# Turning one token tile of the attention weights by VectorE block transposes and small SBUF copies, for seven of eight head pairs

## The chip, the core and the metric

The kernel runs on one core of a Trainium2 chip. The metric is the device time of one execution in microseconds (us). TensorE multiplies, VectorE, ScalarE and GpSimdE work on rows of 128 partitions, SyncE (SP) issues the transfers. On a profile page they are PE (with PEld for its weight loads), DVE, ACT, POOL and SP; L1251 is line 1251 of the kernel.

## The reference

The model has two layers, a pooling mixer and an attention layer, each followed by a squared-ReLU MLP, for 512 tokens of 1024 features. The change is in the attention layer, which has 16 heads of 64:

```
for i in range(S // Q_BLOCK):                 # four blocks of 128 queries
    z = q_blk @ k_blk.T / sqrt(64)            # keys 0 .. 128*(i+1)
    log1m = where(s < t, -softplus(z), 0)
    excl = cumsum_from_the_right(log1m) - log1m
    a = where(s < t, exp(log_sigmoid(z) + excl), 0)
    out_i = a @ v_blk
m = concat(out_i over heads) @ w_o
```

The attention is causal, so the block of queries i meets i+1 blocks of 128 keys: 1 + 2 + 3 + 4 = 10 blocks of 128x128 weights a for each head.

## The kernel before

The 512 tokens are four tiles of 128 (T = 4), the heads eight pairs. For each head the weights of all ten blocks stand side by side in one row of 1280 columns, tokens on the partitions; `SEG` says where a token tile starts: tile 3 (the last one) has columns 0 to 511, tile 2 512 to 895, tile 1 896 to 1151, tile 0 1152 to 1279.

One pair p goes through these steps, named by letters in the list `ATT_ORDER`, which is the order written out by hand for all five engines:

- `S`: 24 score products into six PSUM banks (PE, L1202), three for each head.
- `G`: sigmoids of both heads (ACT, L1216 and L1220).
- `X`, `M` for each head: a scan over the 1280 columns (DVE, L1225), and a multiplication that gives the weights w (DVE, L1316).
- `T` for each head: `transposed` turns the ten blocks w by PE against an identity (L1241), so that keys stand on the partitions, in three PSUM banks, and ACT copies the banks to tiles `at` (L1243).
- `A`: `mix_pair` multiplies v by the turned weights (PE, L1251), both heads side by side in the array, four block rows s of 512, 384, 256 and 128 columns. `a` takes the result out (ACT a cast, then DVE a subtraction, L414 and L415).
- Between them stand `J` and `Q`, the projections of the pair after (24 products each, L842 to L844), `j` and `q`, which split their results in a high part (ACT) and a low part (DVE L415), and work on weights that are loaded late: `L` loads (SP, L223), `g` scales by a gain (DVE, L230), `W` takes the high part (ACT, L249), `w` the low part (DVE, L258). An `L` waits until the `w` that last read its buffer is done, and what stands behind it on SP waits too.

On PE, pair p runs as S(p), J(p+1), Q(p+1), A(p-1), T(p), and then S(p+1). Pair 0 has other work in these places: S0, J1, V4, T0, Q1, V6, where V4 and V6 are products for v (L1126). V6 goes on in the banks of V4, which DVE has to read first (`v4`, L1142). Of DVE's work, `F4` (L1096, L1097 and a split) makes an operand for V6. After pair 6 come S7 and at once A6.

Of the kernel before, what the change touches and what calls it, by code (L numbers as in the profile page):

```python
# [10 lines left out]
F32 = mybir.dt.float32  # L11
# [4 lines left out]
P = 128  # L16
D = 1024
S = 512
T = S // P
KC = D // P  # L20
# [8 lines left out]
PAIRS = HEADS // 2  # L29
WINDOWS = (2, 4, 8, 16)  # L30
EPS = 1e-6
TS = [slice(t * P, (t + 1) * P) for t in range(T)]
NS = [slice(0, 512), slice(512, 1024)]
# [21 lines left out]
ATT_ORDER = [  # L55
    (w[0], int(w[1:2] or 0), int(w[2:] or 0))
    for w in """V5 N2 v5 V0 N3 V3 F3 v0 J0 v3 F2 j0 Q0 L L q0 V1 v1 F1 L L V2 v2
    S0 G0 X00 M00 J1 W X01 w V4 M01 j1 T00 T01 W F4 v4 w Q1 q1 V6 v6
    S1 G1 g g X10 M10 X11 J2 L L M11 W j2 w Q2 q2 A0 a0 T10 T11 W
    S2 G2 g g w X20 M20 X21 J3 M21 W j3 w L L Q3 q3 A1 a1 T20 T21 W  # L60
    S3 G3 g g w X30 M30 X31 J4 M31 W j4 w L L Q4 q4 A2 a2 T30 T31 W
    S4 G4 g g w X40 M40 X41 J5 M41 W j5 w L Q5 q5 A3 a3 T40 T41 W
    S5 G5 w L L X50 M50 X51 J6 M51 W j6 w L Q6 q6 A4 a4 T50 T51 W
    S6 G6 w X60 M60 X61 J7 M61 W j7 w L L L Q7 q7 A5 a5 T60 T61 W
    S7 A6 G7 w L X70 Z002 M70 W X71 w Z102 M71 W T70 w R a6 W w L W Z034 Z134 w T71 L W w L Z055 Z155
    W w L A7 W w Z066 Z166 z206 a7 W w s""".split()
]
# [23 lines left out]
def trunk(ctx, tc, x, consts, gcol, grow, pw, wup, wdn, wq, wk, wv, wo, out):  # L91
    nc = tc.nc
# [9 lines left out]
    def name(s):  # L102
        uid[0] += 1
        return f"{s}{uid[0]}"

    def ps():
        return psum.tile([P, 512], F32, tag="ps", name=name("ps"))
# [13 lines left out]
    turn = [0]  # L121
# [15 lines left out]
    behind, latest = {}, {}  # L137
# [19 lines left out]
    def gains(lo, n):  # L157


        def scaled(raw):  # L160
            for k in range(n):
                c = raw[:, k * D // n : (k + 1) * D // n]
                nc.scalar.mul(c, c, gc[:, lo + k : lo + k + 1])

        return scaled
# [44 lines left out]
    def late_next(what, fits=lambda x: True):  # L210
        while not fits(late[upto[what]]):
            upto[what] += 1
        upto[what] += 1
        return late[upto[what] - 1]
# [8 lines left out]
        nc.sync.dma_start(raw, x["src"])  # L223
        x["raw"] = raw

    def late_scale():
        x = late_next("g", lambda x: x["wide"] is not None)
        c = x["raw"].rearrange("p (k c) -> p k c", k=KC)
        g = gc[:, x["wide"] : x["wide"] + KC].unsqueeze(2).broadcast_to((P, KC, D // KC))
        nc.vector.tensor_tensor(out=c, in0=c, in1=g, op=ALU.mult)  # L230
# [134 lines left out]
    def fill(n=1):  # L365
        if gate[0]:
            behind.update(latest)
        for _ in range(n):
            if queue and sum(map(in_ring, made)) < ahead and (queue[0][0][0] != "dn" or dn_pool[0]):
                if not any(x["key"] == queue[0][0] for x in late) or queue[0][0] in kept:  # L370
                    make()
# [6 lines left out]
    for l in range(2):  # L378
        if l == 1:
            n = len(queue)  # L380
            for what, i, part in ATT_ORDER:
                if what == "V":
                    for h in range(2):
                        at = VALUES[i][2]
# [82 lines left out]
    class Update:  # L467
# [33 lines left out]
        def product(self, n):  # L501
            return self.beside if n and self.cuts is not NS else self.scaled
# [344 lines left out]
    with tc.tile_pool(name="mix0", bufs=1, reuse_waits="tile") as mp:  # L847
# [163 lines left out]
        def transposed(t, h):  # L1011
            pt = pts[t, h] = ps()
            for c in range(4):
                k = 4 * h + c
                nc.tensor.transpose(pt[:, TS[c]], xns[t][:, k * P : (k + 1) * P], ident)
# [47 lines left out]
    with tc.tile_pool(name="att", bufs=1, reuse_waits="tile") as ap:  # L1063
# [164 lines left out]
            )  # L1228
            return e

        def transposed(w):
            parts = {}
            for tiles in ((0,), (1, 3), (2,)):
                pt = ps()
                c = 0
                turned = ap.tile([P, S], F32, tag="at", bufs=6, name=name("at"))
                for s in tiles:
                    parts[s] = turned, c
                    for i in range(s, T):
                        at = SEG[i][0] + s * P  # L1240
                        nc.tensor.transpose(pt[:, c : c + P], w[:, at : at + P], ident)  # L1241
                        c += P
                latest["act"] = nc.scalar.copy(turned[:, :c], pt[:, :c])  # L1243
            return parts

        def mix_pair(p):
            po = pos[p] = ps()
            for s in range(T):
                for a in range(2):
                    turned, c = parts[p, a][s]  # L1250
                    nc.tensor.matmul(  # L1251
                        po[half[a], s * P :], v_all[:, s, 2 * p + a], turned[:, c : c + S - s * P],
                        start=s == 0, stop=s == T - 1, skip_group_check=True,
                    )

        def mixed_out(p):
            if p < PAIRS - 1:
# [24 lines left out]
        with tc.manual_schedule(engines={on.PE, on.Activation, on.DVE, on.Pool, on.SP}):  # L1282
            for what, i, a in ATT_ORDER:
                if what == "V":
                    value_product(i)
                elif what == "v":
                    value_out(i)
                elif what == "F":
                    form(i)
                elif what == "W":  # L1290
                    late_high()
                    if upto["W"] < 16:
                        fill()
                elif what in "Lgws":
                    {"L": late_load, "g": late_scale, "w": late_low, "s": late_store}[what]()
                elif what == "R":
                    gpost1, gpre1 = gain_row(R_MIX_POST1), gain_row(R_MLP_PRE1, spare_tile())
                elif what == "N":
                    need(i)
                elif what in "JQ":  # L1300
                    project(("k" if what == "J" else "q", i))
                    fill()
                elif what == "j":
                    keys(i)
                elif what == "q":
                    queries(i)
                elif what == "S":
                    pzs[i] = scores((qs[i], ks[i]))
                elif what == "G":
                    for a in range(2):  # L1310
                        ws[i, a] = sigmoids(pzs[i], a)
                elif what == "X":
                    es[i, a] = scanned(a)
                elif what == "M":
                    w = ws[i, a]
                    latest["dve"] = nc.vector.tensor_tensor(out=w, in0=w, in1=es.pop((i, a)), op=ALU.mult)  # L1316
                elif what == "T":
                    parts[i, a] = transposed(ws.pop((i, a)))
                elif what == "A":
                    mix_pair(i)  # L1320
                elif what == "a":
                    mixed_out(i)
                elif what in "Zz":
                    out_product(i, range(a // 10, a % 10 + 1), range(2) if what == "Z" else [0])
            assert upto["W"] == upto["w"] == len(late) and not going, upto
            ups = [Update(t, gpost1, None, gpre=gpre1) for t in range(T)]

            def evacuate(t, n):
                up, bank = ups[t], sums.pop((t, n))
                up.halves = (up.halves or []) + [ap.tile([P, 512], F32, tag="at", bufs=6, name=name("at"))]  # L1330
                up.just_square(n, bank)
                latest["dve"] = nc.vector.tensor_tensor(
                    out=up.halves[n], in0=bank, in1=gpost1[:, NS[n]], op=ALU.mult
                )

            for t in range(2):
                for n in range(2):
                    out_product(t, [PAIRS - 1], [n])
                    evacuate(t, n)
                ups[t].factor()  # L1340
            ups[0].sums_added()
            ups[0].rstd()
            ups[1].sums_added()
            ups[0].norm()
            ups[1].rstd()
            ups[1].norm()
            out_product(2, [PAIRS - 1], [0])
            evacuate(2, 0)
            out_product(2, range(PAIRS), [1])
            evacuate(2, 1)  # L1350
            ups[2].factor()
            out_product(3, range(PAIRS - 2), [0])
            ups[0].transpose()
            ups[2].sums_added()
            out_product(3, range(PAIRS - 2, PAIRS), [0])
            out_product(3, [0], [1])
            ups[1].transpose()
            evacuate(3, 0)
            ups[2].rstd()
            ups[2].norm()  # L1360
            out_product(3, range(1, PAIRS), [1])
            fill(4)
            evacuate(3, 1)
            ups[3].factor()
            ups[3].sums_added()
            ups[3].rstd()
            ups[3].norm()
            pending.update({t: ups[t] for t in (T - 2, T - 1)})
# [68 lines left out]
```

## Time and profile before

| | |
|---|---|
| median of 3 runs | 897.04 us (896.95 to 897.58) |
| profiled execution | 896.91 us, its span 895.1 us |
| granted PE clock | 0.999 |
| PE busy | 885.7 us of the span (99%) |
| DVE, ACT busy | 689.4 us, 520.6 us |
| weights turned on PE, all pairs (L1241) | 160 products |
| v times weights (L1251) | 128 products in the trace |

The trace shows a product with 32-bit operands of full precision (the 64 of L1251) as two records. Idle time of an engine that nothing waits for costs nothing: the span is PE's time, and every other engine matters where PE would have to wait for it.

### The profile page before, as it was taken

Reading aid. Unit: us, or ns where it says so; the run is one execution under the profiler, and the core shown is the slowest. Engines: PE = TensorE matmul, PEld = TensorE weight load, DVE = VectorE, ACT = ScalarE, POOL = GpSimd, SP = SyncE. Lnnn points to the kernel's source line nnn. Section 1 sums busy time; section 2 is a strip of 40 time slices with the busy share of each in tenths; the row PEclk is TensorE's granted clock in tenths of the full one; section 3 lists DMA queues with packets and bytes.
Section 4 is the critical chain, followed back from the end, with each engine's and each line's share of the span. In section 5 each row is a group of like instructions: output and inputs, shape, how many; then the busy total and the mean of one; then the engine's idle time right before and its main releaser. Section 6 shows DMA issues by size and latency. Waiting matters only on the chain.

```text
span 895.1 us, 11808 instructions
## 1 busy us (share of the span) xinstructions
PE 885.7 (99%) x4586; PEld 769.4 (86%) x4586; DVE 689.4 (77%) x705; ACT 520.6 (58%) x842; POOL 85.1 (10%) x83
## 2 busy tenths in 40 slices
PE   9999999999999999999999999999999999999996
PEld 7998888888888888888788888998888888888885
DVE  5966897998979967667887784765797776967866
ACT  6758557566888737345577564475445444544531
POOL 2100000000000005000000000120220400303103
PEclk9999999999999999999999999999999999999999
DMA  7453557369796820976122115333415043142102
GB/s 282 160 206 128 192 191 266 117 227 344 275 340 233 313 78 25 366 267 232 51 71 71 48 69 214 118 119 143 140 57 191 35 147 121 51 164 83 56 15 94
DMA packets 42349, 141.00 MB, mean 158 GB/s; under 512 B 4096, under 2 KB 4570, under 8 KB 42294
## 3 DMA queue, kind: packets, MB, share of 16 engines
q1 hardware_dynamic: 42146, 140.24, 43.7%
q8 instruction: 36, 0.59, 0.3%
q14 instruction: 19, 0.16, 0.1%
q10 hardware_dynamic: 148, 0.02, 0.0%
HBM read 116.12 MB, written 24.12 MB: 157 GB/s over the span
## 4 chain that ended last, share of the span: by engine, by line
PE 97%; DMA 1%; issue 1%; DVE 0%; ACT 0%; POOL 0%; POOLq 0%; DVEq 0%; SPq 0%; ACTq 0%
PE ps L726 28%; PE ps L842 16%; PE ps L843 15%; PE ps L844 15%; PE ps L1126 3%; PE ps L455 3%; PE ps L457 3%; PE ps L456 3%; PE ps L1251 2%; PE ps L1241 2%; PE ps L1202 2%; PE ps L981 2%; PE ps L957 1%; PE ps L544 1%; DMA w<-kept 1%
## 5 line engine op out<-in xcount | busy, mean ns | idle before, releaser
L726 PE MATMUL ps<-w,a 128*128 128x512 f32 x1176 | 265.3, 379 | 0.3
L842 PE MATMUL ps<-xnh,w 128*128 128x512 f32 (+1 forms) x704 | 253.5, 362 | 0.0
L844 PE MATMUL ps<-xnh,w 128*128 128x512 f32 (+1 forms) x704 | 253.1, 360 | 0.0
L843 PE MATMUL ps<-xnl,w 128*128 128x512 f32 (+1 forms) x704 | 253.1, 360 | 0.0
L726 PEld LDWEIGHTS ps<-w,a 128*128 128x128 f32 x1176 | 222.1, 189 | 32.5 <-ACT a L414 1.1
L844 PEld LDWEIGHTS ps<-xnh,w 128*128 128x128 f32 x704 | 133.4, 190 | 15.4
L843 PEld LDWEIGHTS ps<-xnl,w 128*128 128x128 f32 x704 | 133.4, 190 | 15.2
L842 PEld LDWEIGHTS ps<-xnh,w 128*128 128x128 f32 x704 | 132.8, 190 | 15.8
L152 ACT CAST w<-raw 128x1024 fp32r<-128x1024 f32 x56 | 58.5, 1045 | 83.9 <-PE ps L844 83.3
L738 DVE TENSOR_TENSOR y<-ps,y 128x512 f32<-128x512 f32 x124 | 83.2, 683 | 30.0 <-PE ps L726 29.9
L154 DVE TENSOR_TENSOR w<-raw,w 128x1024 fp32r<-128x1024 f32 x56 | 69.2, 1237 | 45.5 <-ACT w L152 45.5
L414 ACT CAST w<-e 128x1536 fp32r<-128x1536 f32 (+1 forms) x30 | 41.7, 1391 | 45.9 <-DVE e L699 34.4
L415 DVE TENSOR_TENSOR a<-r,a 128x768 fp32r<-128x768 f32 (+1 forms) x60 | 60.5, 1009 | 0.6 <-ACT a L414 0.6
L415 DVE TENSOR_TENSOR w<-e,w 128x1536 fp32r<-128x1536 f32 (+1 forms) x30 | 50.7, 1691 | 9.7 <-ACT w L414 9.5
L414 ACT CAST a<-r 128x768 fp32r<-128x768 f32 (+1 forms) x60 | 47.1, 785 | 17.9 <-POOL r L680 10.6
L1225 DVE TENSOR_TENSOR_SCAN e<-u,begin 128x1280 f32<-128x1280 f32 x16 | 45.2, 2825 | 13.3 <-ACT u L1216 12.5
L485 POOL TENSOR_TENSOR y<-y,grow 128x512 f32<-128x512 f32 x8 | 12.1, 1510 | 340.7 <-ACT xn L418 340.7
L414 ACT CAST w<-xn 128x1536 fp32r<-128x1536 f32 (+1 forms) x20 | 27.8, 1392 | 24.8 <-PE ps L726 24.8
L415 DVE TENSOR_TENSOR w<-w,w 128x1536 fp32r<-128x1536 f32 (+1 forms) x20 | 34.3, 1713 | 9.0 <-ACT w L414 8.9
L414 ACT CAST w<-w 128x1536 fp32r<-128x1536 f32 (+1 forms) x20 | 27.8, 1392 | 19.2 <-PE ps L726 19.2
L415 DVE TENSOR_TENSOR w<-xn,w 128x1536 fp32r<-128x1536 f32 (+1 forms) x20 | 33.0, 1648 | 7.1 <-ACT w L414 6.9
L761 ACT ACTIVATE r<-ps 128x512 f32<-128x512 f32 x56 | 33.0, 590 | 8.6 <-PE ps L844 8.6
(188 smaller groups left out, 1233.8 us busy)
## 6 DMA issues: line engine op xcount, KB each, us to landing
raw<-in_wup SPq DMA_DIRECT2D x63, 512.0 KB, 3.3
w<-kept SPq DMA_DIRECT2D x42, 512.0 KB, 5.6
w<-in_wdn SPq DMA_DIRECT2D x8, 1536.0 KB, 6.1
xn<-in_wdn SPq DMA_DIRECT2D x16, 768.0 KB, 4.5
kept<-wx SPq DMA_DIRECT2D x20, 512.0 KB, 3.5
kept<-apart SPq DMA_DIRECT2D x16, 512.0 KB, 3.8
apart<-in_wv SPq DMA_DIRECT2D x10, 512.0 KB, 5.1
raw<-in_wdn SPq DMA_DIRECT2D x8, 512.0 KB, 4.3
```

What stands on the lines that cost most here:

```text
L152: nc.scalar.copy(hi, raw)
L154: nc.vector.tensor_tensor(out=lo, in0=raw, in1=hi.bitcast(F32), op=ALU.subtract)
L414: latest["act"] = nc.scalar.copy(hi, src)
L415: latest["dve"] = nc.vector.tensor_tensor(out=lo, in0=src, in1=hi.bitcast(F32), op=ALU.subtract)
L455: nc.tensor.matmul(dst, ah, bh, start=start, stop=False)
L726: nc.tensor.matmul(bank, a[:, x, q, TS[t]], by_twos(w[:, z, q], NS[0]), start=start and q == 0 and k == 0, stop=q == self.n - 1 and k == 2 ...
L738: nc.vector.tensor_tensor(out=part, in0=bank, in1=part, op=ALU.add)
L761: nc.scalar.activation(split_up(r, 256), in_order(pu, 256), ACT.Relu)
L842: nc.tensor.matmul(pu[:, cols], wh[:, k, :], xh, start=k == 0, stop=False)
L843: nc.tensor.matmul(pu[:, cols], wh[:, k, :], xl, start=False, stop=False)
L844: nc.tensor.matmul(pu[:, cols], wl[:, k, :], xh, start=False, stop=k == KC - 1)
L1225: nc.vector.tensor_tensor_scan(out=e[:, ::-1], data0=us[a][:, 1:][:, ::-1], data1=begin[:, ::-1], initial=0.0, op0=ALU.mult, op1=ALU.max,)
```

## The change

For pairs 0 to 6 PE turns only the six blocks of tiles 0 to 2 (three to a bank, two banks a head). The four blocks of tile 3 are turned otherwise. After each `M`, DVE transposes the first 512 columns of w in blocks of 32x32 into a tile `turn` (one buffer). Then 16 transfers (`D`, SP) of 32 partitions by 1 KB carry each block from its row of 32 partitions to the right one in a tile `moved` (one buffer). `mix_pair` multiplies 384, 256 and 128 columns of `at`, and then four times 128 columns of `moved`. Pair 7 stays as it was, but for its tiles. One of the two gain scalings of a row `g g` goes from DVE to ACT (`c`, eight multiplications of 128x128) in pairs 1 to 4. The tiles `at` go from 6 buffers to 4, and the last rows of the layer use the space of v in place of them.

```diff
-    S0 G0 X00 M00 J1 W X01 w V4 M01 j1 T00 T01 W F4 v4 w Q1 q1 V6 v6
-    S1 G1 g g X10 M10 X11 J2 L L M11 W j2 w Q2 q2 A0 a0 T10 T11 W
+    S0 G0 X00 M00 J1 W X01 w V4 M01 j1 T00 T01 W F4 v4 w D0 Q1 q1 V6 v6
+    S1 G1 g X10 M10 X11 J2 L L M11 W j2 c w Q2 q2 A0 a0 T10 T11 D1 W
...
-    S6 G6 w X60 M60 X61 J7 M61 W j7 w L L L Q7 q7 A5 a5 T60 T61 W
+    S6 G6 w X60 M60 X61 J7 M61 W j7 w L L L Q7 q7 A5 a5 T60 T61 D6 W
     S7 A6 G7 w L X70 Z002 M70 W X71 w Z102 M71 W T70 w R a6 W w L W Z034 Z134 w T71 L W w L Z055 Z155
...
+        def turn_blocks(p, a):
+            if a == 0:
+                squares_of[p] = ap.tile([P, 4, 2, T, Q], F32, tag="turn", name=name("turn"))
+            out = squares_of[p][:, :, a].rearrange("p b j q -> p j b q")
+            src = ws[p, a][:, : T * P].rearrange("p (j b q) -> p j b q", b=4, q=Q)
+            latest["dve"] = nc.vector.transpose(out, src)
+
+        def quadrants(p):
+            src, dst = squares_of.pop(p), ap.tile([P, 4, 2, T, Q], F32, tag="moved", name=name("moved"))
+            for row in range(4):
+                for to in range(4):
+                    nc.sync.dma_start(dst[Q * to : Q * to + Q, row], src[Q * row : Q * row + Q, to])
+            return dst
...
-            for tiles in ((0,), (1, 3), (2,)):
+            for group, turned in at_tiles(p, a):
...
+            for s in () if whole else range(T):
+                for a in range(2):
+                    product(a, s, TS[T - 1], moved[p][:, :, a, s], False, s == T - 1)
...
                     latest["dve"] = nc.vector.tensor_tensor(out=w, in0=w, in1=es.pop((i, a)), op=ALU.mult)
+                    if i < PAIRS - 1:
+                        turn_blocks(i, a)
```

The program's order shows it at three places. On PE, the mix of pair 5 and the turning of pair 6 (`at` and `moved` are turned weights, the operand w of an `ident` row is what is turned), before:

```order
L1251 MATMUL ps_4498<-at_4344,v 64x384
L1251 MATMUL ps_4498<-at_4363,v 64x384
L1251 MATMUL ps_4498<-at_4351,v 64x256
L1251 MATMUL ps_4498<-at_4370,v 64x256
L1251 MATMUL ps_4498<-at_4344,v 64x128
L1251 MATMUL ps_4498<-at_4363,v 64x128
L1241 MATMUL ps_4510<-ident,w_4410 128x128 x4
L1241 MATMUL ps_4517<-ident,w_4410 128x128 x4
L1241 MATMUL ps_4524<-ident,w_4410 128x128 x2
L1241 MATMUL ps_4529<-ident,w_4418 128x128 x4
L1241 MATMUL ps_4536<-ident,w_4418 128x128 x4
L1241 MATMUL ps_4543<-ident,w_4418 128x128 x2
```

and after:

```order
L1284 MATMUL ps_4595<-at_4427,v 64x384
L1284 MATMUL ps_4595<-at_4439,v 64x384
L1284 MATMUL ps_4595<-at_4433,v 64x256
L1284 MATMUL ps_4595<-at_4445,v 64x256
L1284 MATMUL ps_4595<-at_4433,v 64x128
L1284 MATMUL ps_4595<-at_4445,v 64x128
L1284 MATMUL ps_4595<-moved_4451,v 64x128 x8
L1275 MATMUL ps_4614<-ident,w_4504 128x128 x3
L1275 MATMUL ps_4620<-ident,w_4504 128x128 x3
L1275 MATMUL ps_4626<-ident,w_4512 128x128 x3
L1275 MATMUL ps_4632<-ident,w_4512 128x128 x3
```

Two products of 512 columns ahead of the first piece have gone (each row of `at` lost 128 columns), eight of 128 columns have come, and 20 turned blocks are 12.

On DVE, pair 0 (w_3308 and w_3316 are the weights of its two heads, e the scans, s the operand for V6, v the rows that `v4` adds to), before:

```order
L1316 TENSOR_TENSOR w_3308<-w_3308,e_3324 128x1280
L1225 SCALAR_TENSOR_TENSOR e_3361<-u_2967,begin 128x1280
L261 SCALAR_TENSOR_TENSOR w_3355<-raw_3192,gc,w_3355 128x512 x2
L1316 TENSOR_TENSOR w_3316<-w_3316,e_3361 128x1280
L415 TENSOR_TENSOR k_3393<-ps_3327,k_3393 128x512
L1096 TENSOR_TENSOR s_3151<-xnh,s_3151 128x1024
L1097 TENSOR_TENSOR s_3151<-s_3151,xnl 128x1024
L415 TENSOR_TENSOR s_3443<-s_3151,s_3442 128x1024
L1142 TENSOR_TENSOR v<-ps_3037,v 128x512
```

and after:

```order
L1364 TENSOR_TENSOR w_3308<-w_3308,e_3324 128x1280
L1244 STREAM_TRANSPOSE turn_3327<-w_3308 128x4x4x32
L1228 SCALAR_TENSOR_TENSOR e_3363<-u_2967,begin 128x1280
L264 SCALAR_TENSOR_TENSOR w_3357<-raw_3192,gc,w_3357 128x512 x2
L1364 TENSOR_TENSOR w_3316<-w_3316,e_3363 128x1280
L1244 STREAM_TRANSPOSE turn_3327<-w_3316 128x4x4x32
L418 TENSOR_TENSOR k_3396<-ps_3329,k_3396 128x512
L1099 TENSOR_TENSOR s_3151<-xnh,s_3151 128x1024
L1100 TENSOR_TENSOR s_3151<-s_3151,xnl 128x1024
L418 TENSOR_TENSOR s_3432<-s_3151,s_3431 128x1024
L1145 TENSOR_TENSOR v<-ps_3037,v 128x512
```

Each multiplication is followed by a transpose of 512 columns, ahead of all that stood behind it.

On SP, the end of pair 6 (the loads are those of `L` in the rows of pairs 6 and 7), before:

```order
L223 DMA spare_4464<-in_wo 128x1024
L223 DMA late_4466<-in_wup 128x1024
L223 DMA raw_4468<-in_wo 128x1024
L223 DMA raw_4608<-in_wo 128x1024
L132 DMA grow_4680<-in_grow 128x1024
```

and after:

```order
L223 DMA spare_4561<-in_wo 128x1024
L223 DMA late_4563<-in_wup 128x1024
L223 DMA raw_4565<-in_wo 128x1024
L1250 DMA moved_4637<-turn_4524 32x256 x16
L223 DMA raw_4720<-in_wo 128x1024
L132 DMA grow_4792<-in_grow 128x1024
```

The 16 transfers of pair 6 stand behind the third load of its row and ahead of the first load of the next.

More of the change, by code (lines that the diff above doesn't have):

```diff
@@ L57 @@
     for w in """V5 N2 v5 V0 N3 V3 F3 v0 J0 v3 F2 j0 Q0 L L q0 V1 v1 F1 L L V2 v2
-    S0 G0 X00 M00 J1 W X01 w V4 M01 j1 T00 T01 W F4 v4 w Q1 q1 V6 v6
-    S1 G1 g g X10 M10 X11 J2 L L M11 W j2 w Q2 q2 A0 a0 T10 T11 W
[L60 to L63, printed above, removed]
-    S6 G6 w X60 M60 X61 J7 M61 W j7 w L L L Q7 q7 A5 a5 T60 T61 W
+    S0 G0 X00 M00 J1 W X01 w V4 M01 j1 T00 T01 W F4 v4 w D0 Q1 q1 V6 v6
+    S1 G1 g X10 M10 X11 J2 L L M11 W j2 c w Q2 q2 A0 a0 T10 T11 D1 W
+    S2 G2 g w X20 M20 X21 J3 M21 W j3 c w L L Q3 q3 A1 a1 T20 T21 D2 W
+    S3 G3 g w X30 M30 X31 J4 M31 W j4 c w L L Q4 q4 A2 a2 T30 T31 D3 W
+    S4 G4 g w X40 M40 X41 J5 M41 W j5 c w L Q5 q5 A3 a3 T40 T41 D4 W
+    S5 G5 w L L X50 M50 X51 J6 M51 W j6 w L Q6 q6 A4 a4 T50 T51 D5 W
+    S6 G6 w X60 M60 X61 J7 M61 W j7 w L L L Q7 q7 A5 a5 T60 T61 D6 W
     S7 A6 G7 w L X70 Z002 M70 W X71 w Z102 M71 W T70 w R a6 W w L W Z034 Z134 w T71 L W w L Z055 Z155
@@ L224, in late_load, with late_scale @@
         x["raw"] = raw
-    def late_scale():
+    def late_scale(on_scalar=False):
         x = late_next("g", lambda x: x["wide"] is not None)
+        if on_scalar:
+            gains(x["wide"], KC)(x["raw"])
+            return
         c = x["raw"].rearrange("p (k c) -> p k c", k=KC)
@@ L1229, in scanned, with at_tiles, transposed @@
             return e
-        def transposed(w):
+        Q = P // 4
+        squares_of, moved = {}, {}
+        def turn_blocks(p, a):
[10 more added lines that the diff above has]
+            return dst
+        def at_tiles(p, a):
+            if p < PAIRS - 1:
+                groups = (((0, T - 2),), ((1, T - 2), (2, T - 2)))
+            else:
+                groups = (((0, T - 1),), ((1, T - 1), (3, T - 1)), ((2, T - 1),))
+            for g, group in enumerate(groups):
+                if g < 2:
+                    yield group, ap.tile([P, S], F32, tag="at", bufs=4, name=name("at"))
+                else:
+                    if a == 0:
+                        moved[p] = ap.tile([P, 2, S], F32, tag="moved", name=name("at"))
+                    yield group, moved[p][:, a]
+        def transposed(p, a, w):
             parts = {}
-            for tiles in ((0,), (1, 3), (2,)):
+            for group, turned in at_tiles(p, a):
                 pt = ps()
                 c = 0
[L1236 to L1239, printed above, removed]
+                for s, last in group:
+                    parts[s] = turned, c, last
+                    for i in range(s, last + 1):
                         at = SEG[i][0] + s * P
@@ L1247, in mix_pair, with product @@
             po = pos[p] = ps()
+            def product(a, s, cols, moving, start, stop):
+                nc.tensor.matmul(
+                    po[half[a], cols], v_all[:, s, 2 * p + a], moving, start=start, stop=stop, skip_group_check=True,
+                )
+            whole = p == PAIRS - 1
             for s in range(T):
                 for a in range(2):
[L1250 to L1254, printed above, removed]
+                    if s in parts[p, a]:
+                        turned, c, last = parts[p, a][s]
+                        cols = slice(s * P, (last + 1) * P)
+                        n = cols.stop - cols.start
+                        product(a, s, cols, turned[:, c : c + n], s == 0, whole and s == T - 1)
+            for s in () if whole else range(T):
+                for a in range(2):
+                    product(a, s, TS[T - 1], moved[p][:, :, a, s], False, s == T - 1)
         def mixed_out(p):
@@ L1293, in trunk @@
                         fill()
+                elif what == "c":
+                    late_scale(True)
+                elif what == "D":
+                    moved[i] = quadrants(i)
                 elif what in "Lgws":
@@ L1316, in trunk @@
                     latest["dve"] = nc.vector.tensor_tensor(out=w, in0=w, in1=es.pop((i, a)), op=ALU.mult)
+                    if i < PAIRS - 1:
+                        turn_blocks(i, a)
                 elif what == "T":
-                    parts[i, a] = transposed(ws.pop((i, a)))
+                    parts[i, a] = transposed(i, a, ws.pop((i, a)))
                 elif what == "A":
@@ L1326, in trunk @@
             ups = [Update(t, gpost1, None, gpre=gpre1) for t in range(T)]
+            gained_rows = ap.tile([P, T, D], F32, tag="v", name="gained")
             def evacuate(t, n):
                 up, bank = ups[t], sums.pop((t, n))
-                up.halves = (up.halves or []) + [ap.tile([P, 512], F32, tag="at", bufs=6, name=name("at"))]
+                up.halves = (up.halves or []) + [gained_rows[:, t, NS[n]]]
                 up.just_square(n, bank)
```

## The prediction

> **What bounds the kernel now.** I read the chain of waits first, then PE around one pair, then the engines that feed it.
>
> ```profile
> PE 97%; DMA 1%; issue 1%; DVE 0%; ACT 0%; POOL 0%; POOLq 0%; DVEq 0%; SPq 0%; ACTq 0%
> ```
>
> PE is 97% of the chain that ends last. So work taken from PE is worth its full length, and each moment in which PE must newly wait costs its full length. The mix of pair 2, the turning of pair 3 and the start of S4 on PE (start, length, name; the next start ends the one before):
>
> ```profile
> 445.08 2.37 PE L1251 MATMUL ps<-at,v 128*64 128x512 f32 x16
> 447.39 2.40 PE L1241 MATMUL ps<-ident,w 128*128 128x128 f32 x20
> 449.72 0.50 PE L1202 MATMUL ps<-k,q 64*128 64x512 f32 x2
> ```
>
> The mix takes 2.31 us, the turning 2.33, or 0.1165 for each block. From mix to mix a pair takes 17.27, by the start of the turning one pair earlier:
>
> ```profile
> 430.13 2.40 PE L1241 MATMUL ps<-ident,w 128*128 128x128 f32 x20
> ```
>
> I call the end of a mix A; here A = 447.39.
>
> **What PE saves.** Seven pairs times two heads times four blocks are 56 blocks times 0.1165: -6.52 us.
>
> **What the mix costs.** Each head has 1280 columns before and after, so the streaming is the same; but 10 passes of 128 columns a pair (five block rows, two passes each) stand where two did. If weight loads set their pace, they are longer. Two such passes are in the trace:
>
> ```profile
> 447.07 0.39 PE L1251 MATMUL ps<-at,v 128*64 128x128 f32 x4
> 447.18 0.28 PE L1251 MATMUL ps<-at,v 128*64 128x128 f32 x2
> ```
>
> The second pass of the two heads starts 0.11 after the first, where streaming asks 0.107 (2.14 us for 1280 columns in two passes). So the lower bound is 0; if each pass takes as long as a turned block, which is also 128 columns, the upper one is 10 x 0.01 = 0.1 a pair. I take 0.05: +0.35 for seven pairs.
>
> **What a transpose costs on DVE.** No row shows a block transpose. The nearest are 512 columns of subtraction, 0.68, and the scan, 2.82 for 1280 columns, which would be 1.13 for 512. A plain move of a column a cycle is nearer to the subtraction: I take 0.68 and keep 1.13 for the range. It reads what the multiplication before it wrote, and so it starts late, as the multiplication does after the scan. DVE in pair 3:
>
> ```profile
> 453.91 2.82 DVE L1225 TENSOR_TENSOR_SCAN e<-u,begin 128x1280 f32<-128x1280 f32 x1 [0.98 <-ACT u L1216]
> 456.87 1.49 DVE L1316 TENSOR_TENSOR w<-w,e 128x1280 f32<-128x1280 f32 x1
> 458.46 2.83 DVE L1225 TENSOR_TENSOR_SCAN e<-u,begin 128x1280 f32<-128x1280 f32 x1
> 461.42 1.49 DVE L1316 TENSOR_TENSOR w<-w,e 128x1280 f32<-128x1280 f32 x1
> 462.83 0.68 DVE L415 TENSOR_TENSOR k<-ps,k 128x512 fp32r<-128x512 f32 x1
> 463.43 1.22 DVE L258 TENSOR_TENSOR w<-spare,w 128x1024 fp32r<-128x1024 f32 x1
> 464.56 0.68 DVE L415 TENSOR_TENSOR q<-ps,q 128x512 fp32r<-128x512 f32 x1
> 465.39 0.69 DVE L415 TENSOR_TENSOR ohl<-ps,ohl 128x512 fp32r<-128x512 f32 x1
> ```
>
> The scan ends at 456.73 and the multiplication starts 0.14 later. The first scan's end is followed by 1.49 and a gap of 0.10 (458.36 to 458.46); k starts 0.08 before the second multiplication ends. With the transpose between, each becomes 0.14 + 0.68 - 0.08 = 0.74: the second head's weights come 0.64 later, and k, w, q and ohl 0.64 + 0.82 = 1.46 later. ACT gives part of it back:
>
> ```profile
> 445.25 0.58 ACT L414 CAST q<-ps 128x512 fp32r<-128x512 f32 x1 [3.70 <-PE ps L844]
> 447.50 0.59 ACT L414 CAST ohl<-ps 128x512 fp32r<-128x512 f32 x1 [1.67 <-PE ps L1251]
> 448.14 2.61 ACT L1243 COPY at<-ps 128x512 f32<-128x512 f32 x6
> 450.57 1.11 ACT L249 CAST w<-raw 128x1024 fp32r<-128x1024 f32 x1
> 451.52 0.66 ACT L1216 ACTIVATE u<-ps 128x511 f32<-128x511 f32 x1
> ```
>
> The six copies hold the sigmoids back, 2.43 us for 2560 columns; 1536 columns take 1.46. So the sigmoids, and the scan behind them, start 0.97 earlier after A. In pairs 1 to 6 DVE's results come 1.46 - 0.97 = 0.49 later after A, while PE's period falls to 17.27 - 0.93 + 0.05 = 16.39.
>
> - The second head's weights: 461.42 + 1.49 is A + 15.52, now A + 15.2. PE wants them six blocks after the next mix, at A + 17.1. Hidden by 1.9.
> - The low part of q: A + 17.85, now A + 18.34. The next S wants it after four products, 0.43 behind its start at A + 16.39 + 1.40 = A + 17.79, so at A + 18.22. About 0.1 late; as a late S also moves what follows it, only some pairs feel it. From 0 to 0.2 for six pairs: +0.4.
> - The gain scaling on ACT: eight of 128x128 took
>
> ```profile
> 227.94 2.44 ACT L163 ACTIVATE apart<-apart,gc 128x128 f32<-128x128 f32 x8
> ```
>
> and ACT is idle for 3.70 before the q cast, where they are put. Nothing.
>
> **Pair 0.** Here no slack of ACT exists: the turning follows M at once, and DVE's list reaches to V6.
>
> ```profile
> 401.76 1.49 DVE L1316 TENSOR_TENSOR w<-w,e 128x1280 f32<-128x1280 f32 x1
> 403.16 0.69 DVE L415 TENSOR_TENSOR k<-ps,k 128x512 fp32r<-128x512 f32 x1
> 403.76 1.22 DVE L1096 TENSOR_TENSOR s<-xnh,s 128x1024 f32<-128x1024 f32 x1
> 405.01 1.22 DVE L1097 TENSOR_TENSOR s<-s,xnl 128x1024 f32<-128x1024 f32 x1
> 407.89 1.23 DVE L415 TENSOR_TENSOR s<-s,s 128x1024 fp32r<-128x1024 f32 x1 [1.66 <-ACT s L414]
> 409.04 0.68 DVE L1142 TENSOR_TENSOR v<-ps,v 128x512 f32<-128x512 f32 x1
> ```
>
> ```profile
> 402.46 2.35 PE L1241 MATMUL ps<-ident,w 128*128 128x128 f32 x20
> ```
>
> The second head's weights end at 403.25, now 403.89. PE is through with the first head's six blocks at 403.16: it waits 0.78 (with 0.05 to see the signal), and ends the turning at 404.64. Q1 runs 5.2 and V6 could start at 409.9.
>
> ```profile
> 406.78 1.08 ACT L414 CAST s<-s 128x1024 fp32r<-128x1024 f32 x1
> 409.87 2.40 PE L1126 MATMUL ps<-w,s 128*128 128x512 f32 x10
> ```
>
> The second sum of F4 ends at 406.23, now 407.69; ACT's cast runs to 408.83, DVE's low part of s to 410.1, and the first addition of `v4`, which V6 has to wait for, to 410.75. V6 waits 0.9. Pair 0: +0.78 + 0.9 = +1.68.
>
> **The 112 transfers.** SP issues them one by one.
>
> ```profile
> 534.03 0.33 SPq L132 DMA_DIRECT2D grow<-in_grow  x1
> 534.41 0.42 SPq L132 DMA_DIRECT2D spare<-in_grow  x1
> ```
>
> ```profile
> L854 ACTq DMA_DIRECT2D row<-in_grow x2: 234/358/483, 1.4 to 2.0; - x2
> ```
>
> Two issues with nothing between stand 0.38 apart for 512 KB each; one of 2 KB still took 0.234. So 32 KB cost between a quarter of it by rows (32 against 128 partitions, 0.1) and 0.38; since the 2 KB one is nearer to the large ones, I take 0.38, 6.1 us for 16. They land in 2.0, as the stores of 256 KB do, and the loads in 3.2:
>
> ```profile
> out<-x SPq DMA_DIRECT2D x7, 256.0 KB, 2.0
> raw<-in_wo SPq DMA_DIRECT2D x5, 512.0 KB, 3.2
> ```
>
> For pairs 0 to 5 the transfers start at about the mix before and have almost a period until their own mix: 6.1 + 2.0 against 16. `turn` is free again at A + 8.2, before the next transpose at A + 10. The loads behind them on SP are issued up to 6 us later; what they bring is first used in the next pair's row. Pair 6 has no period: A6 stands directly behind S7.
>
> ```profile
> 515.23 1.22 DVE L258 TENSOR_TENSOR w<-raw,w 128x1024 fp32r<-128x1024 f32 x1
> ```
>
> ```profile
> 516.51 5.84 SPq L223 DMA_DIRECT2D raw<-in_wo  x2
> ```
>
> ```profile
> 516.45 2.40 PE L1241 MATMUL ps<-ident,w 128*128 128x128 f32 x20
> 518.78 2.14 PE L1202 MATMUL ps<-k,q 64*128 64x512 f32 x24
> 520.85 2.38 PE L1251 MATMUL ps<-at,v 128*64 128x512 f32 x16
> ```
>
> The load at 516.51 waits for the low part that ends at 516.45, when the mix of pair 5 ends too (call that E). DVE's work comes 0.49 later after A and E 0.88 earlier, so this load goes at E + 1.43 and the first copy at E + 1.8. A transfer also waits for the one eight places ahead of it in the rotation of completion signals: the eighth copy waits for this load to land, E + 1.43 + 3.2 = E + 4.63. The 16th is issued eight steps later, E + 7.7, and lands at E + 9.7. PE turns 12 blocks (1.40), does S7 (2.07) and the three pieces from `at` (1.28), and wants `moved` at E + 4.75. It waits 4.9; with issues 0.33 apart 4.5. I take 4.7.
>
> **Sum.** -6.52 + 0.35 + 0.4 + 1.68 + 4.7 = +0.6. Against the profiled execution's 896.91 us (0.13 under the median) this is 897.5.
>
> **Rivals.** 0.2% is 1.8 us, about what a measurement can tell from no change.
>
> - Faster: the small copies are cheap. With 0.08 to issue one and 1.0 to land, the 16th is there at E + 4.63 + 0.6 + 1.0 = E + 6.3, and A6 waits 1.5: 894.3. It decides if the last copy lands before E + 7.1. For it: the copies are a sixteenth of a load and touch no memory outside. Against it: the 0.234 of the 2 KB transfer. 0.25. The Trainium skill speaks for such a case: its page DMA: Bandwidth & Descriptors, in the section "Anatomy of one DMA — SWDGE (gpsimd) path", puts a sequencer's dispatch of a transfer at about 50 ns and the fixed cost of the whole at about 2 us; with both the estimate is a wait of 2.3 and 895.1. The issues in this trace are six times that long, and its stores land in those 2.0.
> - Slower: the transpose runs at the scan's pace, 1.13. Each comes 0.45 later. Pair 0 loses 0.8 more; q is late by 1.0 in each of six pairs, of which half reaches PE, 2.9 more; the load ahead of the last copies moves by 0.9, of which 0.5 shows. 901.7. It decides above about 0.8 for a transpose. Against it: the subtraction's 0.68 for as many columns. 0.2.
> - Slower: the weight loads of the two heads don't overlap, and the short passes take twice 0.1165. 10 x 0.126 less the 0.05 are 1.2 a pair, 8.5 in all: 906. Against it are the 0.11 above. 0.05.
> - A weight load delayed by the copies holds PE up: Q2's load moves from behind Q1 to 6 us later, and should land 1.5 us ahead of its use. 0.05, some 2 us more: 899.5.
>
> **How the numbers follow.** The forecast has 0.45, its own range is 896 to 899: 0.8 of it within 0.2%, 0.1 on either side. Faster is 0.05 and most of the first rival, 0.26; slower 0.05 and the others, 0.33; the same 0.41. The range leaves out about a tenth on each side: 894.0 to 901.3, from the first rival to most of the second.
>
> **What would show it.** On the profile after: about 84 turned blocks for pairs 0 to 6 at 0.1165; transposes of 0.68; PE idle before the second head's turning in pair 0 (0.8) and before V6 (0.9); one wait of 4 to 5 us of PE for `moved` in A6 and none in the other pairs; copies 0.38 apart. I am wrong if the transposes are over 0.8, if the copies stand under 0.2 apart, if PE waits for `moved` in other pairs, or if the mix of a pair takes over 2.5.

## The result, and the profile after

The changed kernel took 913.24 us (median of six runs, 912.65 to 915.64), the kernel before 897.45 beside it on the same chip: ratio 1.0182, 95% interval 1.0168 to 1.0195. It is 15.8 us slower; the forecast was 897.5, with a range up to 901.3. The profiled execution has a span of 910.9 us against 895.1, which are the same 15.8 us, so the two traces can be laid beside each other.

The shares by engine and by line of the chain that ended last, after:

```profile
PE 84%; SPq 6%; DVE 4%; DMA 3%; issue 1%; ACT 1%; POOL 0%; DVEq 0%; POOLq 0%; ACTq 0%
PE ps L729 27%; PE ps L847 13%; PE ps L845 13%; PE ps L846 13%; SPq L1250 6%; PE ps L458 3%; PE ps L459 3%; PE ps L460 3%; PE ps L1129 2%; PE ps L984 2%; DVE e L1228 1%; DMA w<-kept 1%; DMA moved<-turn 1%; PE ps L960 1%; DVE w L1364 1%
```

Where PE had 97% of the chain and SP's queue nothing, the issuing of the copies (L1250) now holds 6% of it. The copies and the transposes, from the views of their two lines (ns, least, median, most):

```profile
L1250 SPq DMA_DIRECT2D moved<-turn x112: 507/589/1480, 410.6 to 533.7; - x112
```

```profile
L1244 DVE STREAM_TRANSPOSE turn<-w x14: 711/711/712, 397.4 to 521.2; 128x512 f32<-128x512 f32 x14
```

A transpose takes 0.71 us. A copy holds SP for 0.59. On SP's timeline (start, length, queue, line) the 16 copies of a pair stand as one row:

```profile
410.58 10.12 SPq L1250 DMA_DIRECT2D moved<-turn  x16
420.75 2.98 SPq L364 DMA_DIRECT2D w<-kept  x6
433.02 10.90 SPq L1250 DMA_DIRECT2D moved<-turn  x16
524.24 10.01 SPq L1250 DMA_DIRECT2D moved<-turn  x16
```

From copy to copy that is 0.63 us, since the last is issued 15 steps after the first and holds SP for 0.59 itself; 16 take 10.0, where the prediction had 6.1. All that PE waited for between 400 and 545 us, and behind it DVE's longest entry (line, what it waited for: sum in us, times, longest):

```profile
PE ps L1284 <- DMA moved<-turn: 8.3, 1, 8.3
PE ps L1205 <- DVE q L418: 4.0, 5, 1.0
PE ps L845 <- DMA w<-kept: 1.3, 1, 1.3
PE ps L1275 <- DVE w L1364: 1.3, 3, 0.6
PE ps L1129 <- DVE v L1145: 0.6, 1, 0.6
PE ps L847 <- DMA w<-kept: 0.6, 1, 0.6
```

```profile
DVE turn L1244 <- DMA moved<-turn: 11.5, 5, 3.1
```

The last row is the one that the prediction excluded. `turn` has one buffer; the next pair's first transpose may write it only when the last copy has read it. On DVE, in pair 2 (start, length, in brackets the idle time before and its releaser):

```profile
441.28 1.49 DVE L1364 TENSOR_TENSOR w<-w,e 128x1280 f32<-128x1280 f32 x1
445.57 0.71 DVE L1244 STREAM_TRANSPOSE turn<-w 128x512 f32<-128x512 f32 x1 [2.80 <-DMA moved<-turn]
```

The copies of pair 1 begin at 433.02 and run 10.90, to 443.92, and the last has still to land: the transpose that was due at 442.77 starts at 445.57. The second scan, the second head's weights and `q` stand behind it, and PE then waits for them:

```profile
446.99 1.52 PE L1284 MATMUL ps<-at,v 128*64 128x384 f32 x12
450.67 0.87 PE L1275 MATMUL ps<-ident,w 128*128 128x128 f32 x6 [0.48 <-DVE w L1364]
453.72 1.67 PE L1205 MATMUL ps<-k,q 64*128 64x512 f32 x20 [1.00 <-DVE q L418]
465.88 1.51 PE L1284 MATMUL ps<-at,v 128*64 128x384 f32 x12
...
525.88 1.51 PE L1284 MATMUL ps<-at,v 128*64 128x384 f32 x12
535.73 1.98 PE L1284 MATMUL ps<-moved,v 128*64 128x128 f32 x16 [8.33 <-DMA moved<-turn]
```

Mix to mix, pair 1 to pair 2, is 18.89 instead of 17.27. In the last row the sixteen pieces from `moved` take 1.98; those of the earlier pairs take 1.04. The granted clock of TensorE says why (stretch, length, PE busy, clock, DMA share, GB/s):

```profile
527.40:535.70 8.30, 0.00 (x0) 0.65 0.21 55
535.70:537.60 1.90, 1.87 (x16) 0.50 0.69 252
537.60:540.40 2.80, 2.80 (x9) 0.55 0.38 124
540.40:545.00 4.60, 4.60 (x23) 1.00 0.42 152
```

After 8.3 us of rest PE works at half clock for 4.4 us, to 540.1. The Trainium skill, in TensorE: Matmul & The Clock Gate, section "HAM oscillation — how this bites in real kernels", says that a rest of over about 3.4 us brings the half clock back; these rows agree, and the prediction had no term for it.

The 15.8 us, by the starts of PE's rows in the two traces:

| term | us | from |
|---|---|---|
| start of pair 0 | -0.3 | T0 starts at 402.18 for 402.46; S0, ahead of every transpose, is as early (389.58 for 389.87) |
| seven pairs without four turned blocks a head | -6.1 | 7 x 0.87, since a pair without a wait takes 16.40 (430.59 to 446.99) for 17.27 |
| row 0: second head's weights, V6 | +1.6 | T0 to S1 takes 13.45 for 12.75, though PE saved 0.87 |
| Q2's weights (`w<-kept`), whose loads stand behind pair 0's copies on SP | +2.35 | S1 to A0 takes 14.96 for 12.61 |
| `turn` held by the copies | +7.4 | A1 to A6 takes 78.89; with two buffers (below) 71.47 |
| A6 waits for its copies | +8.5 | 527.2 to 535.73 |
| slow clock behind that wait | +2.2 | 0.94 in A6, 1.22 up to the third product of Z, the output projection behind it |
| sum | +15.6 | |

### The profile page after: what moved, and what is told of

Its sections match the earlier page's. It is cut to its first block, busy times and chain, and to the rows that moved or that the text cites. A ratio compares the mean times of both kernels' runs of the same rounds, so it can differ in the third digit from the quotient of the medians.

```text
span 910.9 us, 12053 instructions
## 1 busy us (share of the span) xinstructions
PE 885.0 (97%) x4614; PEld 768.6 (84%) x4614; DVE 693.9 (76%) x715; ACT 524.1 (58%) x860; POOL 85.6 (9%) x83
## 4 chain that ended last, share of the span: by engine, by line
PE 84%; SPq 6%; DVE 4%; DMA 3%; issue 1%; ACT 1%; POOL 0%; DVEq 0%; POOLq 0%; ACTq 0%
PE ps L729 27%; PE ps L847 13%; PE ps L845 13%; PE ps L846 13%; SPq L1250 6%; PE ps L458 3%; PE ps L459 3%; PE ps L460 3%; PE ps L1129 2%; PE ps L984 2%; DVE e L1228 1%; DMA w<-kept 1%; DMA moved<-turn 1%; PE ps L960 1%; DVE w L1364 1%
## 5 line engine op out<-in xcount | busy, mean ns | idle before, releaser
L846 PEld LDWEIGHTS ps<-xnl,w 128*128 128x128 f32 x704 | 133.4, 190 | 15.2
```

The source lines that it names most:

```text
L846: nc.tensor.matmul(pu[:, cols], wh[:, k, :], xl, start=False, stop=False)
```

## The experiments

Each was timed against the kernel before on the same chip (896.84, the second four 896.97). In all but the first, a tuple `TURNED` names the pairs that DVE turns and SP's copies carry; the other pairs' blocks are turned by PE, those of the last token tile into `moved`, and `at` is 384 columns wide. Line numbers are up to 5 higher there than in the changed kernel.

**What a copy costs: another form in each pair.** The transfers of each pair were exchanged:

```
-  16 x (32 partitions x 1 KB, block row -> block column)
+  pair 0: d <- s whole       pair 1: dst[:, n] <- src[:, n], n in 0..3
+  pair 2: the same, by halves of 64 partitions
+  pair 3: dst[r, to] <- src[r, to]    pair 4: columns 64n..64n+64
+  pair 5: dst rows <- wup rows        pair 6: 32 x 256 B, then whole
```

> The carried data are not the attention weights here; each pair carries what its 512 KB of blocks would need in another form, so that one run shows what sets the 0.59 us that SP spends on one copy of 32 partitions (0.633 from copy to copy). Pair 0: one transfer of 128 partitions x 4 KB. Pair 1: four of 128 partitions x 1 KB. Pair 2: eight of 64 x 1 KB. Pair 3: sixteen of 32 x 1 KB, each to its own partitions. Pair 4: sixteen of 128 x 256 B. Pair 5: sixteen of 32 x 1 KB from memory outside. Pair 6: sixteen of 32 x 256 B, then one of 128 x 4 KB. Theory A, SP pays for rows: 32 partitions take 0.59 wherever they lie and 128 take some four times that, over 2 us. Theory B, SP pays a fixed sum for a transfer: all of them take about 0.6. Theory C, it pays for crossing partitions: pair 3 comes below pairs 5 and 6 of the changed kernel's form. Theory D, it pays for bytes: pair 6's small ones come to a quarter, and pair 0's one to ten us. The time of the whole isn't looked at.

SP's timeline (the rows of seven pairs, with what was issued behind pair 0's):

```profile
410.56 0.56 SPq L1255 DMA_DIRECT2D moved<-turn  x1
411.23 5.30 SPq L364 DMA_DIRECT2D w<-kept  x6
...
430.65 2.41 SPq L1258 DMA_DIRECT2D moved<-turn  x4
447.07 4.98 SPq L1262 DMA_DIRECT2D moved<-turn  x8
463.46 10.08 SPq L1271 DMA_DIRECT2D moved<-turn  x16
479.88 10.34 SPq L1265 DMA_DIRECT2D moved<-turn  x16
497.98 7.80 SPq L1273 DMA_DIRECT2D moved<-in_wup  x16
515.89 10.06 SPq L1254 DMA_DIRECT2D moved<-turn  x16
527.32 0.51 SPq L1255 DMA_DIRECT2D moved<-turn  x1
```

Theory B holds for copies inside the chip. One transfer of 512 KB held SP for 0.56 and 0.51, one of 128 KB for 0.60, of 64 KB 0.60, of 32 KB 0.59, of 8 KB 0.59 (medians of the lines); rows, bytes and crossing partitions change next to nothing. The source does: the same 32 x 1 KB from memory outside stand 0.49 apart. A source on the chip is not enough, though: the stores of 512 KB in the kernel before (L203) hold SP for a median of 0.33. So the dear ones are the copies with both ends on the chip. The price of carrying a pair goes by its number of transfers; four would have taken 2.4 us where sixteen take 10. In the same run pair 0's single transfer left SP free 9.6 us earlier, PE did not wait in Q2, and its mix started at 428.23 instead of 430.59: Q2's loss is the place of its load behind the copies.

**The transposes alone.** No copies, every block turned by PE, the fourteen transposes kept:

```
+  TURNED = ()
   if i < PAIRS - 1:
       turn_blocks(i, a)
```

> DVE makes its fourteen transposes in their places, but nothing is copied and their output is not used; PE turns every block, as before. It prices the transposes alone. The prediction's terms give +0.4 for q and, in pair 0, +0.64 for the second head's weights and some +0.9 before V6, against 897.4: about 899 (898 to 900). Rival: the transposes, not the copies, are what cost the changed kernel its 16 us: above 904. PE's saving of 6.5 is not in it.

898.17 us, ratio 1.0015 (1.0005 to 1.0024), 1.3 us slower than before. PE's waits between 400 and 545 us are these two, both in pair 0:

```profile
PE ps L1278 <- DVE k L420: 0.4, 1, 0.4
PE ps L1278 <- DVE w L1369: 0.2, 1, 0.2
```

S1 starts 1.30 late, of which 0.42 stand already at S0 (390.29 for 389.87), ahead of the first transpose, so that the transposes cost 0.88. Nothing is lost after it: from pair 1 on the mixes are again 17.26 to 17.29 apart. DVE has the time for its work; the rival falls.

**Two buffers for `turn`.**

```
-  tag="turn", name=name("turn")
+  tag="turn", bufs=2, name=name("turn")
```

> All seven pairs as in the changed kernel, but `turn` has two buffers (the tiles `at` are 384 columns wide to make room, and the last pair's fourth token tile is turned on PE into `moved`). My theory: in pairs 2 to 6 the copies hold the one `turn` until after the next transpose is due, DVE waits 11.5 us for it in all, and PE loses about 7.6 us between A1 and A6 by that. With two buffers DVE no longer waits for `turn`, the pairs keep their 0.9 each, and what is left is pair 0 (Q2's load 2.35), A6 and its clock: about 7 us less than 913.2, so 906 (904 to 908). Rival: the work that a transpose adds on DVE (0.71 twice a pair) makes the low part of q late, whatever `turn` does: no change, 912 to 914, with PE's waits for q still at 0.5 to 1.0.

907.25 us, ratio 1.0112 (1.0095 to 1.0129). PE's waits, all of them:

```profile
PE ps L1287 <- DMA moved<-turn: 8.1, 1, 8.1
PE ps L847 <- DMA w<-kept: 1.2, 1, 1.2
PE ps L849 <- DMA w<-kept: 0.7, 1, 0.7
PE ps L1278 <- DVE w L1369: 0.6, 1, 0.6
PE ps L1131 <- DVE v L1147: 0.6, 1, 0.6
```

The waits for `q` are gone, and three mixes in a row (PE) stand 16.41 and 16.40 apart:

```profile
432.66 1.52 PE L1287 MATMUL ps<-at,v 128*64 128x384 f32 x12
449.07 1.52 PE L1287 MATMUL ps<-at,v 128*64 128x384 f32 x12
465.47 1.52 PE L1287 MATMUL ps<-at,v 128*64 128x384 f32 x12
```

It is 10.4 above the kernel before, where the changed kernel is 15.8 above: a gain of 5.4 for the 7.4 of the table. Most of the rest has a visible cause in the profiled execution: here PE came back from the wait in Q2 at half clock, and S1 to A0 takes 16.67 instead of the 14.96 of the changed kernel, which has the same wait. (That execution took 908.6, the other three 906.4 to 907.88. Its span is only 4.1 shorter than the changed kernel's; behind the attention layer, at L731, it has a wait of 1.3 for DVE that the other trace lacks.)

In all traces the changes of the granted clock lie a whole multiple of 3.413 us apart; here it falls at 426.04 and 525.02 and is back at 429.45 and 535.26. Laid on these intervals, the wait in Q2 of the changed kernel (the first two rows) is cut by a boundary. With two buffers (the last two) it lies in one interval, and the clock falls at that interval's end:

```profile
420.67:424.08 3.41, 2.46 (x12) 1.00 0.70 228
424.08:427.49 3.41, 2.51 (x11) 1.00 0.96 359
422.63:426.04 3.41, 1.54 (x7) 1.00 0.88 333
426.04:429.45 3.41, 3.39 (x8) 0.50 0.98 360
```

**Pair 6 turned by PE.** One buffer for `turn`, as in the changed kernel:

```
+  TURNED = (0, 1, 2, 3, 4, 5)
```

> Pairs 0 to 5 as in the changed kernel; pair 6 is turned by PE, as all pairs were. My theory: the wait of A6 for `moved` (8.33) and the slow clock behind it (some 2.2) go, and so does DVE's wait for `turn` in pair 6 (about 1 on PE), and its saving of 0.93 is lost: 913.2 - 8.3 - 2.2 - 1.1 + 0.9 = 902.5 (901 to 904), and the clock granted behind S7 is that of before. Rival: the end is held by the late loads of the output weights behind the copies on SP, and A6's wait only hides that: then the first products of Z wait instead, and the time stays above 907.

902.1 us, ratio 1.0063 (1.0048 to 1.0079), as expected. After A5 no wait of PE is left. What remains are the losses of row 0, Q2 and `turn`; three waits for `q` have 1.0 us each. The profiled execution took 904.74 with two stretches of half clock, behind Q2's wait and from 474.44; the other three took 901.45 to 902.12 at a mean granted clock of 0.997 to 0.999 for 0.993, which leaves room for neither.

**The mix of pair 6 later.** Two buffers for `turn`, all seven pairs, and in the table of the order:

```
-  S7 A6 G7 w L X70 Z002 M70 W X71 w Z102 M71 W T70
+  S7 G7 w L X70 Z002 M70 W X71 w Z102 A6 M71 W T70
```

> The form with two buffers for `turn`, and the mix of pair 6 moved in the table from directly behind S7 to behind Z102: 36 products of the output (some 7.8 us of PE) now stand between S7 and it. My theory: A6's wait of 8.06 was only the 16 issues with nothing to do beside them, and the slow clock behind it (the moved part 1.97 instead of 1.04, slow products after it, some 2.2 in all) follows from PE's rest. Both go: 907.25 - 8.1 - 2.2 = 897.0 (896 to 898.5). Rival: the wait only changes its name (the output products then wait for their weights or for banks), time above 903. Second rival: the clock falls for another reason than the rest, and its 2.2 stay: 899.

896.49 us, ratio 0.9996 (0.9986 to 1.0005): 10.8 below the same kernel with the mix in its old place. SP issued the copies as slowly as ever; PE had other work in that time:

```profile
529.30 1.52 PE L1287 MATMUL ps<-at,v 128*64 128x384 f32 x12
530.90 1.09 PE L1287 MATMUL ps<-moved,v 128*64 128x128 f32 x16
```

The moved part is back at 1.09, so wait and slow clock go together. The clock followed the rest.

**The copies issued by POOL.** Two buffers for `turn`, the mix of pair 6 in its old place.

```
-  nc.sync.dma_start(dst[...], src[...])
+  nc.gpsimd.dma_start(dst[...], src[...])
```

> The form with two buffers for `turn`, and the 112 copies issued by POOL instead of SP, with POOL idle in this stage. If the 0.63 us from copy to copy belong to SP alone, POOL's copies come faster, A6 waits 2 or less, and Q2's load on SP is on time again: 907.25 - 2.3 - 6 - 2.2, about 897. If a transfer costs its issuer some 0.6 on any queue, only Q2's load comes back: 907.25 - 2.3 = 905. If POOL takes over 1 us for a copy, A6 waits 16 or more, and copies of one pair run into the next: above 912.

902.88 us, ratio 1.0063 (1.0048 to 1.0079): 4.4 below the form with SP, near the second case, with Q2's load (2.35) and the half clock behind it (1.7) back. POOL's timeline in the last pair:

```profile
513.36 3.23 POOL L1252 DMA_DIRECT2D moved<-turn  x6 [5.48 <-PE ps L1287]
517.86 2.69 POOL L1252 DMA_DIRECT2D moved<-turn  x5 [1.27 <-issue]
521.36 0.50 POOL L1252 DMA_DIRECT2D moved<-turn  x1 [0.81 <-issue]
522.21 2.13 POOL L1252 DMA_DIRECT2D moved<-turn  x4 [0.35 <-issue]
```

POOL too pays some half a microsecond for a copy, with pauses between: 11.0 us for 16. A6 still waits, 7.75. The price is that of a transfer, on either queue; SP's own loss was what stood behind the copies.

**Only where it is hidden.** Two buffers for `turn`, and in the second also the late mix of pair 6:

```
+  TURNED = (1, 2, 3, 4, 5)
+  TURNED = (1, 2, 3, 4, 5, 6)
```

> Pairs 1 to 5 alone are turned by DVE and carried, `turn` with two buffers; pairs 0, 6 and 7 are turned by PE. My theory: each of these pairs gives 0.88 (17.27 against the 16.40 from mix to mix with two buffers), and none of the three losses (row 0, Q2's load, A6) is left: 896.84 - 5 x 0.88 = 892.4 (891.5 to 893.5), faster than before. Rival: the first carried pair always delays the loads behind it, so that D1 makes Q3's load late as D0 made Q2's: 894.5. Second rival: no gain, 896 to 898, if the pairs' 0.88 is taken back at the end.

> Pairs 1 to 6 turned by DVE and carried, `turn` with two buffers, the mix of pair 6 behind Z102. My theory, if the late mix costs nothing: 896.84 - 6 x 0.88 = 891.6 (890.7 to 893). Rival: the late mix has a price of its own (banks held, the output's weights later on SP behind D6's copies), and the time is at or above that of pairs 1 to 5 alone, 892.4 or more.

892.59 us, ratio 0.9952 (0.9939 to 0.9964), and 892.37 us, 0.9948 (0.9935 to 0.996): both faster than the kernel before by 0.5%. In the second PE waits for nothing between 400 and 545 us. The sixth pair brings 0.6 in the span (890.4 against 891.0) and 0.2 in the medians, less than the measurement tells apart, of the 0.88 that I gave it. Its late mix has a small gap, as in the run above, where the moved part starts 1.60 after the part from `at` instead of 1.35.

## Why the prediction was wrong

The step that failed is the price of a transfer: "since the 2 KB one is nearer to the large ones, I take 0.38, 6.1 us for 16", with 0.38 as the upper end. Measured are 0.63 and 10.0. The error was in the bound: I let the loads, which come from memory outside, cap a copy from one on-chip buffer to another, a kind of transfer of which that trace had no row; the 0.234 of the small one, too, stood on ACT's queue. Of the 15.2 us between forecast and result, `turn` has 7.4, A6 3.8, Q2's load 2.35 and PE's clock 2.2; the other terms together give a few tenths back. The price runs through three later steps:

- "`turn` is free again at A + 8.2, before the next transpose at A + 10": with ten microseconds of issuing it is free at about A + 12, two too late. The cover was gone, and the pairs lost 7.4 that had no term. The run with two buffers took the waits for `q` away.
- "The loads behind them on SP are issued up to 6 us later": they were issued 10 later, and Q2's load came too late. This stood as the last rival, with 0.05 and 2 us; it cost 2.35.
- A6, "I take 4.7": 8.5. The first copy goes at E + 3.0 (521.26 to 524.24) instead of E + 1.8, since the transpose before it had waited for `turn`, and the sixteenth lands at E + 14.2 instead of E + 9.7. With two buffers the first goes at E + 1.6, and the wait is still 8.1: most of the miss is the issuing itself. That the eighth copy waits for a load to land played no part.

One loss was not in the sum under any name: PE's half clock after a long rest, 2.2 us.

What held:

- PE saves 6.52 and the mix costs 0.35: together -6.17, measured -6.1. The sum is right by luck: both terms were too large, and the errors mostly cancel. Twelve blocks take 1.46 (432.91 to 434.37) where twenty took 2.33, so a pair saves 0.87 and not 0.93: the 0.1165 was an average with the start of a turning in it, which stays. And the mix takes 2.32 (430.59 to 432.91) for 2.31, so the short passes cost 0.01 a pair and not 0.05.
- The transpose: 0.68, measured 0.71; the rival with the scan's pace falls.
- The low part of `q`, +0.4: nothing. Where `turn` is free the mixes stand 16.40 apart, and the transposes alone cost pairs 1 to 6 nothing. The 4.0 us of waits for `q` in the changed kernel came from `turn`.
- Pair 0, +1.68: 1.57. By the starts, the second head's weights cost 0.81 (forecast 0.78) and V6 0.75 (forecast 0.9).
- The forecast's falsifier "if PE waits for `moved` in other pairs" stayed false: only A6 did. The damage went through the write side of the buffer, by which no falsifier looked.

Two things stay open. One is why a copy inside the chip holds its issuer longer than a load or a store. The other is how much rest makes PE's clock fall. That it falls at the end of an interval of 3.413 us, so that the place of a wait in the interval counts, is read from the traces. The page on TensorE in the Trainium skill (TensorE: Matmul & The Clock Gate, section "What's actually happening") names a window of 3413 ns that runs freely; the traces agree with the length. The amount does not come out of them: ahead of a fall PE was busy for 1.54 of 3.41 us in the rows above and for 2.39 in another kernel (471.03 to 474.44, pair 6 turned by PE), but it was busy for 2.39 too in an interval of the changed kernel without a fall behind it (451.39 to 454.80). No run moved a wait across a boundary and nothing else.

## What to carry to other kernels

Price a transfer of a kind that the trace doesn't hold by its count first, and keep the upper bound open: sixteen small copies of 32 KB held their issuer for 10.0 us, one of 512 KB for 0.56. When a queue's time per stage is uncertain, ask for each buffer when its last reader ends, not only when its content arrives; here a second buffer was worth 5.4 us. A step with no work beside it belongs where there is some: moving one mix behind independent products gave back a wait of 8 us and the slow clock after it, and with the second buffer in place, leaving out the two pairs without cover turned a loss of 1.1% into a gain of 0.5%.

## What the runs showed of the hardware

- SP's time for a transfer inside the chip did not depend on its size: 0.51 to 0.60 us from 8 KB to 512 KB, on POOL 0.50. The Trainium skill, in DMA: Bandwidth & Descriptors, section "Anatomy of one DMA — SWDGE (gpsimd) path", gives about 50 ns for the sequencer's dispatch of a transfer that GpSimd issues. Of the times that the runs show for an issue none is near it, POOL's 0.50 included; the 1.8 us to landing do fit its 2 us for a whole transfer.
- The half clock also came after rests far shorter than 3.4 us. With pair 6 turned by PE a wait of 1.0 us for `q` at 473 was followed by 3.4 us at half clock, 474.44 to 477.85:

```profile
472.00:474.00 2.00, 1.11 (x4) 1.00 0.12 33
474.00:478.00 4.00, 3.87 (x23) 0.57 0.18 49
```

In that execution two other waits for `q` of the same length were followed by no such stretch in its S products (1.68 and 1.66 us for twenty, against 2.69 here). In these traces a short wait of PE cost between itself and 1.7 us more, the 1.7 behind the wait in Q2.
